# A decoder block on one core: the modulation loads of the projection stage move from SyncE's queue to GpSimd's, and a memset moves from GpSimd to VectorE

## The chip, the cores and the metric

The kernel runs on one core of one Trainium2 chip. The core has five engines with an instruction queue each: TensorE (PE in the profile; its weight loads are PEld), VectorE (DVE), ScalarE (ACT), GpSimd (POOL) and SyncE (SP). A DMA is asked for by one of the engines and carried out by 16 DMA engines. The metric is the device time in microseconds of one execution; for the kernel before it is the median of three runs.

## The reference

One layer of a hybrid decoder, 512 tokens of width 2048, all in fp32:

```python
mod = silu(c) @ w_ada + b_ada                  # six rows of 2048: shift1, scale1, gate1, shift2, scale2, gate2
h = rms_norm(x, norm1_w) * (1 + scale1) + shift1
aq, ak, av, gq, gf, gi, gg = split(h @ w_in)   # seven groups of 1024 columns
attn = rms_norm(dilated_attention(rope(norm(aq)), rope(norm(ak)), av), attn_out_norm_w)
hg = rms_norm(hgrn2(gq, gf, gi, lb), hg_norm_w) * silu(gg)
x = x + gate1 * (concat(attn, hg) @ w_out)
h2 = rms_norm(x, norm2_w) * (1 + scale2) + shift2
x = x + gate2 * (square(relu(h2 @ w_ff1)) @ w_ff2)
```

`hgrn2` is a gated linear recurrence over the tokens with 8 heads of 128 channels: its forget factors f multiply up along the tokens. The modulation `mod` is a product of one vector with a matrix of 2048 by 12288, 100 MB of weights that are read once.

## The kernel before

**Stages.** The norm of x and its scale come first, beside a first group of columns of w_in. Then the shift, then the input projection, in groups of 512 columns, with attention and the recurrence fitted between its matmuls. Then the output projection, the first products of the MLP, and two long stages with a fast matrix product. Weights come as fp32 in tiles of two k rows (`wraw`, 512 KB, L189). ScalarE rounds each to a high part (`whi`, L39), VectorE takes the rest (`wlo`, L40), and TensorE multiplies three times.

**Modulation.** One block of 512 columns of a modulation row is a `gemv` (L116): 16 loads of 128 by 512 from `w_ada` (256 KB each, tile `araw`, L123), each followed by a multiply and add on VectorE into one of two sums (`acc`, L127 and L129). `to_cols` (L138) adds the two sums (L143), lets TensorE transpose them (L149), and ScalarE sums the transposed rows. In the first stage the tiles come from pools of that stage (`early`). Later `araw` has four buffers of its own and `acc` two. `shift_through` (L744) is a gemv of `w_in` with the shift, which adds the shift's part to columns that were projected without it.

**What sets the order.** The gemvs are Python generators in a list `bgw`. `project` (L368) calls `bg_step` 1.85 times for each k of a projection, and each call writes the next load with its sum into the program. The list holds, after L836: `shift_through` of the forget gate's second half, then gate1 (`mod_rows(2)`, four gemvs), then scale and shift of the second norm (`mod_cols(4)` and `mod_cols(3)`, four each), 13 gemvs with 208 loads. gate2 (`mod_rows(5)`, L896) comes in the output projection. The order of TensorE's instructions from L831 on is that of the program. On all other engines a planner orders the instructions by simulated times, the program's order being their priority; an instruction may be put far ahead of its place in the program if its buffer is free. On the chip each engine takes its instructions in the order so fixed, so that one that waits holds up those behind it. A load waits until VectorE has read the last tile that stood in its buffer.

**The recurrence.** `hgrn_head` (L577) works through levels L = 1, 2, 4 to 256. A level multiplies z, S and f on VectorE (L597 to L608), and TensorE multiplies the z of a level (L574, L648 and others). `Sx` is S, with 512 columns, taken as pairs of halves of L columns. For L = 1 GpSimd sets all of `Sx` to 1 (L604), and VectorE copies f's odd columns over the even ones (L605). The odd columns keep the 1. There are eight heads.

**GpSimd's other work in this stage.** The rotations of q and k (L422 to L424, in `qk_norm`) and the powers for the norms (L212). In the first stage it asks for small constants, and its power for the norm of x (`rx`) is one step to the first matmuls. From the output projection on it asks for DMAs of x1 (L931) and of the MLP's operands (L1027, L1066, L1122).

Of the kernel before, what the change touches and what calls it, by code (L numbers as in the profile page):

```python
# [44 lines left out]
def hybrid_block(ctx, tc, x, c, positions, norm1_w, w_ada, b_ada, w_in, q_norm_w, k_norm_w,  # L45
                 attn_out_norm_w, hg_lb_logits, hg_norm_w, w_out, norm2_w, w_ff1, w_ff2,
                 lnc, hgmask, inv_freq, out):
    nc = tc.nc
    pe, dve, act, pool = nc.tensor, nc.vector, nc.scalar, nc.gpsimd
# [66 lines left out]
    def gemv(view, vec, col0, n=512, early=False):  # L116

        accs = [(work("acc") if early else gv.tile([P, 512], F32, name="acc"))[:, 0:n] for _ in range(2)]
        nk = 512 // n
        for k0 in range(0, NK, nk):  # L120
            raw = spare.pop(0) if early and spare else slot("araw") if early else gv.tile([P, 512], F32, name="araw", bufs=4)
            raw = raw.rearrange("p (k n) -> p k n", n=n)
            nc.sync.dma_start(raw, view[:, k0:k0 + nk, col0:col0 + n])  # L123
            for k in range(k0, k0 + nk):
                acc = accs[k % 2]
                if k < 2:
                    dve.tensor_scalar(acc, raw[:, k - k0], vec[:, k:k + 1], None, op0=ALU.mult)  # L127
                else:
                    dve.scalar_tensor_tensor(acc, raw[:, k - k0], vec[:, k:k + 1], acc, op0=ALU.mult, op1=ALU.add)  # L129
            yield  # L130
        gemv.acc = accs

    def run_all(g):
        for _ in g:
            pass
        return gemv.acc
# [23 lines left out]
    def mod_cols(kind, b, dst, nw, n=512, early=False):  # L160

        for _ in gemv(ada_v, sc, kind * D + b * n, n, early):
            yield
        nb = n // P
        d = dst[:, b * nb:(b + 1) * nb]
        yield from to_cols(gemv.acc, d)
        dve.tensor_tensor(d, d, bcol[:, kind * NK + b * nb:kind * NK + (b + 1) * nb], op=ALU.add)
        if nw is not None:
            mod_cols.last = dve.scalar_tensor_tensor(d, d, 1.0, nw[:, b * nb:(b + 1) * nb], op0=ALU.add, op1=ALU.mult)
        yield  # L170
# [39 lines left out]
    def rstd_of(dst, ss, n, inv_n):  # L210
        dve.tensor_scalar(dst, ss, inv_n, EPS, op0=ALU.mult, op1=ALU.add)
        pool.tensor_tensor(dst, dst, mhalf[:, 0:n], op=ALU.pow)  # L212
# [15 lines left out]
    def slot(name, dt=F32):  # L228
        return io.tile([P, 512], dt, name=name, tag="io")

    def work(name, dt=F32):
        return wk.tile([P, 512], dt, name=name, tag="wk")
# [113 lines left out]
    def bg_step():  # L346

        while bgw:
            try:
                return next(bgw[0])  # L350
            except StopIteration:
                bgw.pop(0)
# [85 lines left out]
    def qk(c0, name, i):  # L438
        ts = evac(project(c0, tok_mm), name)
        rs = sm.tile([P, NT, 4], F32, name=f"rs{i}", bufs=2)  # L440
        bgw.insert(0, qk_norm(ts, i, rs))
        return ts if i else (ts, rs)
# [134 lines left out]
    def hgrn_head(h, f, q, vs, ss):  # L577
# [7 lines left out]
        Sx = work("Sx")  # L585
        near = sm.tile([P, 4, 32], F32, name="near", bufs=2)

        def level(L):

            with tc.high_priority(offset=400):  # L590
                return level_ops(L)

        def level_ops(L):
            n = S // (2 * L)
            z = work("z")
            zv, kv, qv, pv, sv = (t.rearrange("p (n u l) -> p n u l", u=2, l=L) for t in (z, kk, q, f, Sx))
            if L == 1:  # L597
                dve.tensor_copy(zv[:, :, 0], kv[:, :, 0])
            else:
                dve.tensor_tensor(zv[:, :, 0], kv[:, :, 0], sv[:, :, 0], op=ALU.mult)  # L600
            dve.tensor_tensor(zv[:, :, 1], qv[:, :, 1], pv[:, :, 1], op=ALU.mult)
            if L < 256:
                if L == 1:
                    pool.memset(Sx, 1.0)  # L604
                    dve.tensor_copy(sv[:, :, 0], pv[:, :, 1])  # L605
                else:
                    dve.tensor_tensor(sv[:, :, 0], sv[:, :, 0], pv[:, :, 1, L - 1:L].broadcast_to([P, n, L]), op=ALU.mult)
                dve.tensor_tensor(pv[:, :, 1], pv[:, :, 1], pv[:, :, 0, L - 1:L].broadcast_to([P, n, L]), op=ALU.mult)  # L608
            return z
# [79 lines left out]
    def hgrn(fs, qs, vs, rs):  # L689
        ss = sm.tile([P, 4, NT], F32, name="hss", bufs=2)  # L690
        for h in range(4):
            yield from hgrn_head(h, fs[h], qs[h], vs, ss)
        rstd_of(rs.rearrange("p t h -> p (t h)"), ss.rearrange("p t h -> p (t h)"), 16, 1.0 / DH)
# [50 lines left out]
    def shift_through(col0):  # L744

        yield from gemv(win_v, s1c, col0, early=col0 < 4096 + 512)
        col = sm.tile([P, 8], F32, name="scol", bufs=2)
        yield from to_cols(gemv.acc, col[:, 0:4])
        for h in range(4):
            if col0 == 3072:  # L750
                dve.tensor_scalar(col[:, 4 + h:5 + h], col[:, h:h + 1], QS, None, op0=ALU.mult)
                sg = wk.tile([P, 512], F32, name="sg", tag="ev", bufs=2)
                act.activation(sg, hq0[h], AF.Sigmoid, scale=1.0 / QS, bias=col[:, h:h + 1])
                dve.scalar_tensor_tensor(hq0[h], hq0[h], col[:, 4 + h:5 + h], sg, op0=ALU.add, op1=ALU.mult)
            else:
                f, hd = ((f0, h), (f1, 4 + h))[(col0 - 4096) // 512]
                forget(hd, f[h], f[h], col[:, h:h + 1])
        yield
# [75 lines left out]
    while bgw:  # L834
        bg_step()
    bgw[:] = later  # L836
    tasks.append(hgrn(f0, hq0, hv0, hrs[0]))
    q0 = qk(0, "aq", 0)
    k0_ = qk(1024, "ak", 1)
# [13 lines left out]
    tasks.append(hg_out(1, gs, f1, hrs[1]))  # L853
    while bgw:
        bg_step()


    def project_out(q, rate, after):
# [542 lines left out]
def _program(arrays):  # L1401
    import concourse.bacc as bacc
    nc = bacc.Bacc("TRN2", target_bir_lowering=False, num_devices=1)
    args = [nc.dram_tensor(n, a.shape, mybir.dt.from_np(a.dtype), kind="ExternalInput").ap()
            for n, a in arrays.items()]
    args.append(nc.dram_tensor("out_0_dram", _OUTS[0][0], F32, kind="ExternalOutput").ap())
    with tile.TileContext(nc, schedule_with_timeline_sim=True) as tc:
        hybrid_block(tc, *args)
    return nc
# [10 lines left out]
```

## Time and profile before

| what | value |
|---|---|
| median of 3 runs | 2297.67 us (2294.38 to 2297.95) |
| the profiled execution | 2297.95 us, of which the trace's span is 2296.2 us |
| granted TensorE clock, mean of the span | 0.996 of full speed |
| the changed line's loads from w_ada, all stages | 384 of 256 KB, median 4.3 us from issue to landing |
| memsets of L604 | 8, from 194.2 to 636.6 us |
| TensorE busy, 500 to 600 us | 99.77 of 100 us |
| TensorE busy, 600 to 700 us | 96.78 of 100 us |

The profile is of one execution. A row of a group gives the line, the engine, the operation, the tile written and the tiles read, shapes and count, then busy time in us and mean duration in ns, then the idle time of the engine just ahead of these instructions with what ended it. A row of waits gives who waited for whom, the sum in us, how often, and the longest. A row of a timeline gives the start, the length, the engine and the instruction, with the idle time before it in brackets. SPq is SyncE's queue: its rows are instructions that ask for DMAs. In the chain of waits, which is followed back from the last instruction, a DMA's row has its issue and its time to landing.

### The profile page before, as it was taken

Reading aid. Unit: us, or ns where it says so; the run is one execution under the profiler, and the core shown is the slowest. Engines: PE = TensorE matmul, PEld = TensorE weight load, DVE = VectorE, ACT = ScalarE, POOL = GpSimd, SP = SyncE. Lnnn points to the kernel's source line nnn. Section 1 sums busy time; section 2 is a strip of 40 time slices with the busy share of each in tenths; the row PEclk is TensorE's granted clock in tenths of the full one; section 3 lists DMA queues with packets and bytes.
Section 4 is the critical chain, followed back from the end, with each engine's and each line's share of the span. In section 5 each row is a group of like instructions: output and inputs, shape, how many; then the busy total and the mean of one; then the engine's idle time right before and its main releaser. Section 6 shows DMA issues by size and latency. Waiting matters only on the chain.

```text
span 2296.2 us, 33105 instructions
## 1 busy us (share of the span) xinstructions
PE 2224.9 (97%) x11769; PEld 1824.4 (79%) x11769; DVE 1809.9 (79%) x2765; ACT 1098.2 (48%) x1950; POOL 447.3 (19%) x664
## 2 busy tenths in 40 slices
PE   4899999999999999999999999999999999999999
PEld 3787877888778888778887888888888888888887
DVE  6999777677876565668648988988897679967878
ACT  5555434433344454447544556555564333343332
POOL 1000022000230000002232323323332222222221
PEclk9999999999999999999999999999999999999999
DMA  9798455556545256746969799889889987998784
GB/s 327 254 335 315 124 177 156 177 160 207 187 151 184 68 173 225 247 152 217 367 231 383 251 344 347 298 306 386 298 328 390 339 293 260 385 344 291 278 301 164
DMA packets 262582, 598.31 MB, mean 261 GB/s; under 512 B 23220, under 2 KB 43968, under 8 KB 262416
## 3 DMA queue, kind: packets, MB, share of 16 engines
q1 hardware_dynamic: 186800, 332.54, 43.1%
q0 software_dynamic: 70720, 254.21, 30.0%
q10 hardware_dynamic: 4896, 9.44, 1.2%
q8 instruction: 93, 1.52, 0.3%
q14 instruction: 73, 0.60, 0.1%
HBM read 518.49 MB, written 77.61 MB: 260 GB/s over the span
## 4 chain that ended last, share of the span: by engine, by line
PE 60%; DVE 17%; DMA 14%; issue 6%; ACT 2%; POOL 1%; SPq 0%; DVEq 0%; ACTq 0%; POOLq 0%
PE f L1177 9%; PE f L1178 9%; PE f L1176 9%; DMA araw<-in_w_ada_dram 6%; PE prj L198 5%; PE prj L199 5%; PE prj L200 5%; DVE vlo L1161 3%; DVE acc L129 3%; DVE raw L1144 2%; PE f L208 2%; PE f L206 2%; PE f L207 2%; DMA Fl<-f_lod 2%; DVE wlo L40 2%
## 5 line engine op out<-in xcount | busy, mean ns | idle before, releaser
L1160 ACT CAST vhi<-raw 128x1024 fp32r<-128x1024 f32 x392 | 413.4, 1055 | 534.5 <-PE f L1178 416.3
L1161 DVE TENSOR_TENSOR vlo<-raw,vhi 128x1024 fp32r<-128x1024 f32 x392 | 475.5, 1219 | 153.5 <-ACT vhi L1160 152.7
L1177 PE MATMUL f<-vlo,Fh 128*128 128x512 f32 x1376 | 537.1, 390 | 3.9 <-DVE vlo L1161 3.8
L1178 PE MATMUL f<-vhi,Fl 128*128 128x512 f32 x1376 | 535.8, 389 | 0.8 <-DMA Fl<-f_lod 0.8
L1176 PE MATMUL f<-vhi,Fh 128*128 128x512 f32 x1376 | 536.1, 390 | 0.0
L39 ACT CAST whi<-wraw 128x512 fp32r<-128x512 f32 (+1 forms) x368 | 219.8, 601 | 453.2 <-PE prj L200 313.3
L198 PE MATMUL prj<-whi,hi 128*128 128x512 f32 x896 | 364.9, 407 | 1.3 <-ACT gg L701 1.3
L200 PE MATMUL prj<-whi,lo 128*128 128x512 f32 x896 | 351.4, 392 | 0.0
L199 PE MATMUL prj<-wlo,hi 128*128 128x512 f32 x896 | 351.0, 392 | 0.0
L40 DVE TENSOR_TENSOR wlo<-wraw,whi 128x512 fp32r<-128x512 f32 (+1 forms) x368 | 243.2, 665 | 120.9 <-ACT whi L39 118.3
L129 DVE SCALAR_TENSOR_TENSOR acc<-araw,sc,acc 128x512 f32<-128x512 f32 (+1 forms) x392 | 252.7, 672 | 100.5 <-DMA araw<-in_w_ada_dram 99.2
L1177 PEld LDWEIGHTS f<-vlo,Fh 128*128 128x128 f32 x1376 | 258.3, 188 | 63.3 <-DVE vlo L1161 10.0
L1178 PEld LDWEIGHTS f<-vhi,Fl 128*128 128x128 f32 x1376 | 258.3, 188 | 54.8 <-DMA Fl<-f_lod 1.6
L1176 PEld LDWEIGHTS f<-vhi,Fh 128*128 128x128 f32 x1376 | 258.3, 188 | 53.5
L1144 DVE TENSOR_TENSOR raw<-raw,raw 128x1024 f32<-128x1024 f32 x224 | 267.7, 1216 | 4.1 <-DMA raw<-in_w_ff_dram 3.9
L198 PEld LDWEIGHTS prj<-whi,hi 128*128 128x128 f32 x896 | 169.3, 189 | 36.5 <-ACT gg L701 1.6
L200 PEld LDWEIGHTS prj<-whi,lo 128*128 128x128 f32 x896 | 168.9, 188 | 36.7
L199 PEld LDWEIGHTS prj<-wlo,hi 128*128 128x128 f32 x896 | 169.5, 189 | 33.0 <-DVE wlo L40 1.0
L1122 POOL DMA_DIRECT2D Fh<-f_hid x112 | 79.0, 705 | 425.9 <-PE f L1178 410.8
L208 PE MATMUL f<-hi,wlo 128*128 128x512 f32 x256 | 99.8, 390 | 1.3 <-DVE wlo L40 1.3
L206 PE MATMUL f<-hi,whi 128*128 128x512 f32 x256 | 100.2, 391 | 0.0
L207 PE MATMUL f<-lo,whi 128*128 128x512 f32 x256 | 99.6, 389 | 0.0
(311 smaller groups left out, 2917.0 us busy)
## 6 DMA issues: line engine op xcount, KB each, us to landing
raw<-in_w_ff_dram SPq DMA_DIRECT2D x224, 512.0 KB, 9.7
araw<-in_w_ada_dram SPq DMA_DIRECT2D x384, 256.0 KB, 4.3
Fh<-f_hid POOLq DMA_DIRECT2D x112, 512.0 KB, 6.5
Fl<-f_lod POOLq DMA_DIRECT2D x112, 512.0 KB, 7.7
wraw<-in_w_in_dram SPq DMA_DIRECT2D x104, 512.0 KB, 4.1
Fh<-h_hid POOLq DMA_DIRECT2D x60, 512.0 KB, 6.6
Fl<-h_lod POOLq DMA_DIRECT2D x60, 512.0 KB, 7.5
f_hid<-part POOLq DMA_DIRECT2D x48, 512.0 KB, 7.9
```

Of the source, the lines that this page charges most:

```text
L39: nc.scalar.copy(hi, src)
L40: (eng or nc.vector).tensor_tensor(lo, src, hi.bitcast(F32), op=ALU.subtract)
L129: dve.scalar_tensor_tensor(acc, raw[:, k - k0], vec[:, k:k + 1], acc, op0=ALU.mult, op1=ALU.add)
L198: pe.matmul(banks[ti], lhsT=hi[:, ts], rhs=whi, start=first, stop=False)
L199: pe.matmul(banks[ti], lhsT=hi[:, ts], rhs=wlo, start=False, stop=False)
L200: pe.matmul(banks[ti], lhsT=lo[:, ts], rhs=whi, start=False, stop=last)
L1144: dve.tensor_tensor(dst, a, b, op=ALU.subtract)
L1160: act.copy(hi, src)
L1161: split_done.append(dve.tensor_tensor(lo, src, hi.bitcast(F32), op=ALU.subtract))
L1176: pe.matmul(banks[t], lhsT=fh[u][a][:, ts], rhs=whi[:, a], start=first, stop=False)
L1177: pe.matmul(banks[t], lhsT=fh[u][a][:, ts], rhs=wlo[:, a], start=False, stop=False)
L1178: pe.matmul(banks[t], lhsT=fl[u][a][:, ts], rhs=whi[:, a], start=False, stop=end)
```

## The change

The queue that asks for a gemv's loads becomes a variable. It is SyncE's at first, GpSimd's from the point where the list of gemvs is exchanged (after the projection that ends at L835), and SyncE's again after the list is empty (L855). And in the first level of a recurrence head VectorE writes the odd columns of `Sx`, 256 of 512, in place of GpSimd's memset of all 512.

```diff
@@ gemv
-            nc.sync.dma_start(raw, view[:, k0:k0 + nk, col0:col0 + n])
+            gemv.queue.dma_start(raw, view[:, k0:k0 + nk, col0:col0 + n])
...
+    gemv.queue = nc.sync
@@ level_ops
                 if L == 1:
-                    pool.memset(Sx, 1.0)
+                    dve.memset(sv[:, :, 1], 1.0)
                     dve.tensor_copy(sv[:, :, 0], pv[:, :, 1])
@@ the projections
     while bgw:
         bg_step()
     bgw[:] = later
+    gemv.queue = pool
     tasks.append(hgrn(f0, hq0, hv0, hrs[0]))
...
     while bgw:
         bg_step()
+
+    gemv.queue = nc.sync
```

The weight loads (L189) stay on SyncE, and so does the store of a modulation row (L183).

## The prediction

> **What bounds the kernel now.** I read the page first, for the shares of the whole run:
>
> ```profile
> PE 2224.9 (97%) x11769; PEld 1824.4 (79%) x11769; DVE 1809.9 (79%) x2765; ACT 1098.2 (48%) x1950; POOL 447.3 (19%) x664
> ```
>
> TensorE (PE) works 97% of the span, so this change can only be worth what TensorE waits for. Next I asked for one line's instructions, those of L123, to see when the loads of the change run, and cut the other views to that stretch, 270 to 770 us:
>
> ```profile
> L123 SPq DMA_DIRECT2D araw<-in_w_ada_dram x184: 327/328/985, 276.7 to 741.4; - x184
> DMA to landing us min/median/max: 2.5/3.4/5.6
> 270.00:770.00 500.00, 489.24 (x3758) 397.03 (x3757) 377.64 (x844) 217.47 (x655) 70.82 (x108) 1.00 0.55 170
> ```
>
> The third row is a stretch: its length, then busy time of PE, PEld, DVE, ACT and POOL, the clock, the share of the DMA engines and GB/s. TensorE is idle for 10.8 of the 500 us. The clock is full and the DMA engines are at 55%, so neither is short. GpSimd (POOL) works 71 us. The waits of the stretch, TensorE's first, then VectorE's (DVE), then SyncE's queue:
>
> ```profile
> PE pC L648 <- DVE z L601: 3.8, 3, 2.8
> PE pB L574 <- DVE z L601: 3.5, 2, 2.4
> PE ptq L454 <- ACT p_sb L492: 2.7, 2, 2.0
> PE pD L665 <- DVE z L601: 0.4, 1, 0.4
> DVE acc L129 <- DMA araw<-in_w_ada_dram: 63.3, 53, 3.1
> SPq L189 <- DVE wlo L40: 90.6, 42, 12.4
> SPq L123 <- DVE acc L129: 81.4, 125, 2.3
> ```
>
> TensorE waits 7.7 us (3.8 + 3.5 + 0.4) for z of the recurrence, which VectorE writes. VectorE itself stands 63.3 us in 53 waits for the very loads that the change moves, and the z queue behind such a wait. One case, from VectorE's timeline, SyncE's timeline and the chain of waits:
>
> ```profile
> 382.60 0.75 DVE L129 SCALAR_TENSOR_TENSOR acc<-araw,sc,acc 128x512 f32<-128x512 f32 x1 [2.30 <-DMA araw<-in_w_ada_dram]
> 377.06 1.13 SPq L189 DMA_DIRECT2D wraw<-in_w_in_dram  x1
> 378.29 4.28 DMA araw<-in_w_ada_dram
> 521.73 2.55 DMA araw<-in_w_ada_dram
> 664.81 2.66 DMA araw<-in_w_ada_dram
> ```
>
> The load of 378.29 is asked for right behind a weight load (377.06) and takes 4.28 us, and VectorE stands 2.30 us for it. Two that were asked for with no weight load ahead took 2.55 and 2.66. From these two facts I take a rate for the whole argument: 7.7 us of TensorE's time per 63.3 us of VectorE's, 0.12 us per us. It is an estimate that all z waits come from such stands.
>
> One cover is wide. The sums of a gemv must be done when TensorE, whose order is by hand, comes to their transposes. Of the 12 gemvs between 289 and 765 us this is the tightest:
>
> ```profile
> 515.69 0.68 DVE L143 TENSOR_TENSOR acc<-acc 128x512 f32<-128x512 f32 x1
> 525.07 0.60 PE L149 MATMUL pc<-ident,acc 128*128 128x128 f32 x4
> ```
>
> The sum ends at 516.37 and is used at 525.07, so a gemv may come 8.7 us later at no cost. Lateness hurts only through what queues on VectorE behind a load.
>
> **The change part by part.** By the code 208 loads move: 16 of the forget gate's shift (L828), 64 of gate1 (L726), 128 of the second norm's scale and shift (L727 to L729). The loads of gate2 (L896) and the shift loads before L834 stay on SyncE.
>
> *Issue.* SyncE sheds 208 x 0.328 = 68 us. I cost that at nothing: its queue in the wait view stands behind VectorE (81.4 us for the slot of the next load, 90.6 us for a weight slot), not behind its own issuing, and no row of TensorE names a weight load. GpSimd takes the issuing over. The nearest row is its own 256 KB DMA at L931:
>
> ```profile
> L931 POOL DMA_DIRECT2D x1d<-x x16: 539/539/651, 875.3 to 1022.6; - x16
> DMA to landing us min/median/max: 2.6/5.8/7.7
> wraw<-in_w_in_dram SPq DMA_DIRECT2D x68, 512.0 KB, 4.0
> ```
>
> That is 208 x 0.54 = 112 us more on an engine with 429 of 500 us free, and 0.54 - 0.33 = 0.2 us later for each load.
>
> *Landing.* Bounds: every load as quick as one alone and 0.2 later, 2.8 against the median of 3.4, or every one as slow as the median of L931, 5.8. Over 53 stands that is -32 to +127 us for VectorE, and by the rate -3.8 to +15 us for TensorE. I take a value near the low end, since L931 writes to memory amid other stores, and its fastest (2.6) is as quick as SyncE's fastest (2.5). A load in a queue of its own no longer stands behind a weight load: I put it at 3.8, between 4.28 and the 2.6 of one alone and nearer the weight load's own 4.0, because the weight bytes still pass beside it. If half of the loads gain 0.5 and the other half lose 0.2, the mean is -0.15 us, 53 x 0.15 = 8 us of VectorE, **-1.0 us**. The Trainium skill ("DMA: Bandwidth & Descriptors", section "Queues, rings and completion order") has each DMA engine take its queues in turn, a packet at a time; by that a 256 KB load would share with the weight load and not queue behind it, which is the gaining half of this term and no more. In this trace weights and modulation rows are all in one queue, so it cannot show that.
>
> *Waiting in GpSimd's queue.* A load that waits for its slot now holds up what stands behind it on GpSimd: the rotations of q and k, their powers and those of the norms. Their users come late (scores start after the next projection), so that is free up to the length of a projection. The other way round, a load waits for GpSimd's own work:
>
> ```profile
> L422 POOL TENSOR_TENSOR rot<-aq,rot_w 128x64 f32<-128x64 f32 x32 | 12.9, 436 | 56.2 <-ACT aq L406 55.9
> L212 POOL TENSOR_TENSOR hrs<-hrs,mhalf 128x16 f32<-128x16 f32 x2 | 5.8, 2898 | 67.4 <-DVE hrs L211 67.4
> L604 POOL MEMSET Sx<- 128x512 f32 x6 | 3.2, 526 | 224.8 <-PE pT L490 89.2 <-ACT whi L39 60.0 <-DVE AT L642 38.5
> 641.76 7.52 POOL L422 TENSOR_TENSOR rot<-ak,rot_w 128x64 f32<-128x64 f32 x8 [4.68 <-ACT ak L406]
> 658.60 3.36 POOL L212 TENSOR_TENSOR rs<-rs,mhalf 128x16 f32<-128x16 f32 x1
> ```
>
> Without the memsets GpSimd is busy 70.8 - 3.2 = 67.6 of 500 us, so 14% of the loads meet it: 7 of the 53 that VectorE stands for. If the order on GpSimd interleaves the two, such a load is late by an operation or a few, 0.4 to 3.4 us; I take 1.4, which makes 10 us of VectorE, **+1.2 us**. Bounds: 0, where the planner puts loads ahead, and the rival below.
>
> *The memset.* GpSimd loses eight of 0.53 us, and with them a stand of 224.8 us in front of them behind which loads would queue; that is what the second half of the edit takes away. VectorE gains eight writes of 256 elements. No such row exists; the nearest is the copy of the same shape, and the bounds are VectorE's quickest groups and an operation with two inputs of that shape:
>
> ```profile
> L605 DVE COPY Sx<-f 128x256 f32<-128x256 f32 x6 | 1.8, 307 | 0.0
> L127 DVE TENSOR_SCALAR acc<-araw,sc 128x512 f32<-128x512 f32 x23 | 11.2, 485 | 8.2 <-PE pc L149 7.3 <-DMA araw<-in_w_ada_dram 0.7
> ```
>
> 8 x 0.31 = 2.5 us of VectorE, beside 122 us in which it is idle: **+0.3 us**, at most 2.5 (if every z then is late by it), not below 0, as nobody waited for the memset (the instructions of L604 list no one).
>
> The Trainium skill ("SBUF — State Buffer", sections "SBUF: two separate sides" and "A bandwidth-pool intuition that's wrong") speaks against the change: while VectorE runs a one-input fp32 operation within SBUF, GpSimd cannot write descriptors, and a DMA of 620 ns came to 3,100. Here L605 and L127 are of that kind, 13 of 500 us, 2.6%, so 5.4 of the 208 loads would be 2.5 us late, an estimate from that page's figures: 13 us of VectorE, 1.6 of TensorE, and a time of 2301.2 and not 2299.6. The row of L931 (539 typical, 651 at most) shows none of it, and I leave it out of the sum.
>
> *The first four.* The slots for these loads are free from the start, and the planner uses that already: it asks for four rows of w_in at 36 us which nothing reads for 100 us.
>
> ```profile
> 36.06 2.85 SPq L123 DMA_DIRECT2D araw<-in_w_in_dram  x4
> 12.70 0.48 POOL L97 DMA_DIRECT2D rows<-in_hg_norm_w_dram  x1
> 27.48 1.21 POOL L212 TENSOR_TENSOR rx<-rx,mhalf 128x4 f32<-128x4 f32 x1 [14.29 <-DVE rx L211]
> 13.98 5.62 DMA xs<-in_x_dram
> 19.61 5.42 DMA xs<-in_x_dram
> 50.00:60.00 10.00, 8.04 (x38) 6.48 (x37) 10.00 (x27) 6.87 (x16) 0.00 (x0) 1.00 1.09 354
> ```
>
> On GpSimd the first free place is after 13 us, while it waits for rx, and there the DMA engines carry the x tiles on the chain. Four loads take 2.85 us of them, so the start can be 2.85 later. They leave SyncE at 36 us, but what follows then is paced by VectorE (10.00 of 10.00 at 50 us) as much as by DMA, so little is won back. Between no cost and all of it I take the middle: **+1.4 us**. A gain is not excluded where VectorE is not full, and -2.85 is the far end.
>
> The sum is -1.0 + 1.2 + 0.3 + 1.4 = +1.9 on the profiled execution (2297.95 us, 0.28 above the median of 2297.67). On the median that makes **2299.6 us**, no difference that this kernel's runs can show (they tell 0.2%, 4.6 us, from nothing).
>
> **The rivals.** *A, the stands go.* With a queue of its own a load is asked for ahead and lands alone, VectorE no longer stands, and TensorE's 7.7 us for z go: 2297.67 - 7.7 = 2290.0. For it: three of the four rows of waits name z. Against it: SyncE's stand of 81.4 us is for VectorE to free a slot, which another queue does not shorten.
>
> *B, GpSimd's order is the new wait.* If the planner puts a run of rotations ahead of loads that are due, the loads wait for the whole run, and first for q itself (55.9 us of waits in two runs). The run from 641.76 to 661.96 is 20.2 us; the four runs are 67.6 - 5.8 = 61.8 us. Each us is a stand of VectorE, which works in order: 61.8 x 0.12 = 7.4, with the first four 2297.67 + 7.4 + 1.4 = 2306.5. It decides where such a wait passes the 8.7 us that a gemv has in hand, for then TensorE stands for its transposes as well. Against it: the planner orders GpSimd by the same simulated time as the others, and most runs are short pieces with places between them.
>
> *C, nothing moves.* The loads are paced by VectorE's slots in both kernels and come at the same times: 2297.7. It cannot be told from my forecast by time, and its chance is in it.
>
> **How the numbers follow.** Forecast with C: 0.48. A: 0.27, with what lies between, over 0.2% faster. B: 0.25, over 0.2% slower. Besides the priced terms the new queues give the planner other times, and VectorE's order in the stretch changes with them; the 10.8 us that TensorE idles there may become a few more or less, which both rivals hold. The range is from a little beyond A to a little beyond B, 2288 to 2308; of the bounds it leaves out the far end of the landing (+15), which would need every load as slow as a store beside other stores.
>
> **What would show it.** Right: 208 DMAs of L123 on GpSimd at about 0.54 us, a landing of 3.3 to 3.7 us, VectorE's wait for them at 45 to 75 us in 270 to 770, and TensorE idle 9 to 14 us there. The first four stand before 27 us on GpSimd, and TensorE's first full stretch starts 0 to 3 us later. For A the z rows are gone. For B waits of L123 behind rotations or aq stand in the list of GpSimd's waits, and TensorE waits for acc at L149. Wrong I would be if the order of VectorE or ScalarE changed before 270 us, where TensorE has little in hand, by more than these terms.

## The result, and the profile after

The kernel after takes 2313.5 us (median of 6 runs, 2308.8 to 2314.5) against 2297.8 (6 runs beside them, 2294.4 to 2302.3). The ratio on record is 1.0059, 95% interval 1.0047 to 1.0070: slower by 13.6 us, between 10.8 and 16.1. Effects in this text are those of the ratio; the two medians by themselves differ by 15.7 us. The time is beyond the range of the prediction. The profiled execution took 2313.01 us, its span is 2311.2. Lines behind `gemv` stand two lower than before (L143 is now L145).

TensorE has the same work and a lower share; GpSimd is busy 102 us more. The columns are engine, busy time in us, its share of the span and the number of instructions:

```profile
PE 2227.8 (96%) x11769; PEld 1826.3 (79%) x11769; DVE 1819.1 (79%) x2773; ACT 1098.3 (48%) x1950; POOL 549.7 (24%) x864
```

Of the 15.0 us between the two spans, 12.1 are idle time of TensorE (span less busy time, 83.4 against 71.3), and 2.9 are busy time for the same instructions, at a granted clock of 0.994 against 0.996 in the mean. So most of the loss is waiting, and a smaller part is slower work.

The stretch of the recurrence comes some 15 us later, so its views are cut to 280 to 790 us. First the loads by their line, then the stretch as one row (columns as in the prediction):

```profile
L123 POOL DMA_DIRECT2D araw<-in_w_ada_dram x184: 538/538/766, 289.0 to 761.8; - x184
DMA to landing us min/median/max: 2.8/3.7/7.9
```

```profile
280.00:790.00 510.00, 493.75 (x3773) 400.18 (x3772) 388.05 (x858) 219.44 (x659) 160.78 (x286) 0.99 0.54 167
```

A load is issued in 0.54 us and lands 3.7 us after its issue began, 0.3 later than from SyncE; 0.2 of that is the longer issue. TensorE stands 16.3 of 510 us, where it stood 10.8 of 500. The waits of the stretch, TensorE's, VectorE's and GpSimd's:

```profile
PE pC L650 <- DVE z L603: 8.3, 4, 3.9
PE pB L576 <- DVE z L603: 3.8, 2, 2.2
PE pD L667 <- DVE z L603: 0.8, 1, 0.8
PE pC L656 <- DVE z L603: 0.2, 1, 0.2
DVE acc L129 <- DMA araw<-in_w_ada_dram: 70.7, 60, 3.8
POOL araw L123 <- DVE acc L129: 155.6, 101, 5.5
POOL araw L123 <- DVE acc L127: 123.1, 16, 47.6
```

TensorE's waits for z went from 7.7 to 13.1 us. GpSimd stands for VectorE to free a slot, as SyncE did before. So some 5 us arise in this stretch. The greater part is ahead of it. To see where, I set the k-th matmul of each kind in the one trace beside the k-th in the other; the table gives how much later it begins (median of the 25 matmuls from that time on, us) by its time in the trace of before:

| at (us) | 28 | 92 | 140 | 212 | 320 | 400 | 540 | 690 | 900 | 1400 | 2200 |
|---|---|---|---|---|---|---|---|---|---|---|---|
| after | 2.7 | 4.2 | 4.2 | 12.0 | 13.5 | 9.1 | 8.9 | 19.5 | 18.5 | 16.0 | 15.0 |

There are two steps ahead of 220 us: 4.2 us in the start and 8 us between 170 and 212. After that it goes up and down: down by 4 us to 400 us, up by 10 in the recurrence, and down by 4 to the end.

**The first step.** GpSimd's timeline in the start, and SyncE's load of the x tiles, after:

```profile
7.07 1.67 POOL L123 DMA_DIRECT2D araw<-in_w_in_dram  x3
10.09 0.54 POOL L123 DMA_DIRECT2D araw<-in_w_in_dram  x1 [1.35 <-DMA rw<-in_k_norm_w_dram]
30.16 1.21 POOL L214 TENSOR_TENSOR rx<-rx,mhalf 128x4 f32<-128x4 f32 x1 [16.33 <-DVE rx L213]
```

```profile
7.63 15.73 SPq L257 DMA_DIRECT2D xs<-in_x_dram  x16
```

The same of SyncE before:

```profile
7.52 13.09 SPq L255 DMA_DIRECT2D xs<-in_x_dram  x16
```

The four loads of w_in stand at 7 to 10 us, beside the x tiles. SyncE needs 2.64 us longer to get its 16 x tiles asked for, and the power for the norm of x comes at 30.16, 2.68 us later than before.

**The second step.** TensorE's stands at the end of the shift, before and then after:

```profile
214.17 1.11 PE L149 MATMUL pc<-ident,acc 128*128 128x128 f32 x4 [4.86 <-DVE acc L143]
```

```profile
202.89 0.50 PE L201 MATMUL prj<-wlo,hi 128*128 128x512 f32 x1 [3.64 <-DVE wlo L40]
226.17 1.11 PE L151 MATMUL pc<-ident,acc 128*128 128x128 f32 x4 [7.54 <-DVE acc L145]
```

The stands of after sum to 11.2 us, 6.3 more than that of before; the rest of the 8 us is not in stands of TensorE. It waits longer for sums of the shift, so I followed these sums on VectorE back to where they begin. TensorE's and VectorE's timelines at 105 to 145 us, before:

```profile
113.78 0.22 PE L769 MATMUL ps_v<-ident,posf 4*128 4x4 f32 x1
```

```profile
125.41 0.20 DVE L818 TENSOR_SCALAR cosT<-rp 128x64 f32<-128x64 f32 x1
128.49 0.54 DVE L127 TENSOR_SCALAR acc<-araw,sc 128x512 f32<-128x512 f32 x1
```

And after:

```profile
109.53 0.27 PE L770 MATMUL ps_v<-ident,rows 128*128 128x128 f32 x1
126.09 0.22 PE L771 MATMUL ps_v<-ident,posf 4*128 4x4 f32 x1
```

```profile
126.35 0.20 DVE L772 COPY cols<-ps_v 128x41 f32<-128x41 f32 x1 [0.84 <-PE ps_v L771]
141.04 0.20 DVE L820 TENSOR_SCALAR cosT<-rp 128x64 f32<-128x64 f32 x1
141.16 1.06 DVE L127 TENSOR_SCALAR acc<-araw,sc 128x512 f32<-128x512 f32 x2
```

`ps_v` (L770, L771) is a pair of small transposes, of the small vectors and of the positions, from which VectorE makes the table of the rotations (to `cosT`). Before, TensorE does them one behind the other at 113.6 to 114 us. After, the second stands behind more of the projection, at 126 us. The table follows 15.6 us later on VectorE, and the shift's next gemv (L127), which stands behind the table in VectorE's order, begins at 141.16 and not at 128.49. VectorE is then busy all of the time from 150 to 200 us in both kernels (25.00 of 25.00 in the windows 150:175 and 175:200), so nothing of that is made good before TensorE comes to the sums. That the late table is the cause is so far an argument from the order; e5_psv_first tries it.

### The profile page after: what moved, and what is told of

The parts are those of the page before. It is cut to its first block, busy times and chain, and to the rows that moved or that the text cites. A ratio compares the mean times of both kernels' runs of the same rounds, so it can differ in the third digit from the quotient of the medians.

```text
span 2311.2 us, 33191 instructions
## 1 busy us (share of the span) xinstructions
PE 2227.8 (96%) x11769; PEld 1826.3 (79%) x11769; DVE 1819.1 (79%) x2773; ACT 1098.3 (48%) x1950; POOL 549.7 (24%) x864
## 4 chain that ended last, share of the span: by engine, by line
PE 61%; DVE 14%; DMA 13%; issue 8%; POOL 2%; ACT 1%; SPq 0%; DVEq 0%; POOLq 0%; ACTq 0%
PE f L1182 11%; PE f L1183 11%; PE f L1181 11%; DMA araw<-in_w_ada_dram 8%; PE prj L200 4%; PE prj L202 4%; PE prj L201 4%; DVE vlo L1166 3%; DVE acc L129 2%; PE f L210 2%; PE f L208 2%; PE f L209 2%; DVE raw L1149 2%; DVE wlo L40 1%; PE prj L209 1%
## 5 line engine op out<-in xcount | busy, mean ns | idle before, releaser
L129 DVE SCALAR_TENSOR_TENSOR acc<-araw,sc,acc 128x512 f32<-128x512 f32 (+1 forms) x392 | 254.8, 676 | 108.5 <-DMA araw<-in_w_ada_dram 107.3
L123 POOL DMA_DIRECT2D araw<-in_w_ada_dram x192 | 105.0, 547 | 367.4 <-DVE acc L129 185.1
```

## The experiments

Theory T1: the loss comes from the first gemv of the list, whose loads run ahead into the start, and from the order that the planner then makes (T1a: through the late table; T1b: through the gemv's other 12 loads). Rival T2: from GpSimd's queue in the recurrence, by later landings and by standing in order. Rival T3: from VectorE, by the write that it got and by any change of its order. Times are medians of 5 to 12 runs beside 23 to 35 of before; intervals are those of the ratio. The table gives the shift of the matmuls against before, as above, of the profiled executions:

| at (us) | 28 | 92 | 140 | 212 | 320 | 400 | 540 | 690 | 900 | 1400 | 2200 | ratio (95%) |
|---|---|---|---|---|---|---|---|---|---|---|---|---|
| e1_memset | 0.4 | 0.7 | 0.7 | 0.6 | 0.7 | 1.3 | 1.4 | 4.3 | 2.9 | 3.0 | 3.9 | 1.0007 (0.9995 to 1.0019) |
| e2_queue | 2.8 | 4.2 | 4.2 | 12.8 | 14.7 | 10.7 | 9.7 | 13.8 | 12.5 | 17.1 | 17.0 | 1.0058 (1.0041 to 1.0075) |
| e3_first_sp | -0.2 | 0.1 | 0.4 | 0.4 | 0.6 | -3.4 | -4.1 | 3.6 | 2.9 | 5.3 | 8.4 | 1.0016 (1.0005 to 1.0028) |
| e4_held | -0.4 | -0.8 | -0.8 | 4.1 | 4.7 | 0.3 | 0.1 | 5.2 | 4.5 | 1.1 | 1.8 | 1.0026 (1.0014 to 1.0037) |
| e5_psv_first | 2.9 | 3.6 | 3.5 | 3.3 | 3.6 | -1.3 | -2.0 | 8.3 | 8.3 | 5.8 | 4.7 | 1.0022 (1.0006 to 1.0037) |
| e6_first4 | 2.5 | 3.5 | 3.5 | 9.1 | 9.0 | 11.0 | 13.2 | 15.9 | 14.7 | 13.6 | 13.3 | 1.0035 (1.0022 to 1.0048) |
| e7_other12 | 0.4 | -0.3 | -0.3 | -0.5 | -0.3 | 1.1 | 2.6 | 2.8 | 1.4 | 0.5 | 2.5 | 1.0005 (0.9992 to 1.0019) |
| e9_first2 | 1.9 | 1.5 | 1.5 | 10.6 | 12.1 | 11.0 | 11.2 | 10.9 | 9.8 | 9.7 | 8.6 | 1.0040 (1.0028 to 1.0052) |

One execution differs from the next by some us, which add up along the span, so the columns to 320 us are read first, and for the end the ratio.

### The memset alone (e1_memset)

The kernel before, with:

```diff
-                    pool.memset(Sx, 1.0)
+                    dve.memset(sv[:, :, 1], 1.0)
```

> The kernel before with the second half of the edit alone: VectorE writes the odd columns of Sx, all modulation loads stay on SyncE. Theory T1 (the 15 us come from the first gemv of the list, whose loads run ahead into the start and whose place changes VectorE's order between 90 and 220 us; the stage of the recurrence adds some 7 us that are given back in part): no part of that is here, 2297 to 2300 us, with TensorE's matmuls at the times of before up to 270 us. Rival T2 (GpSimd's queue in the recurrence itself: landings 0.35 us later, loads in order behind each other): the same 2297 to 2300. Rival T3 (VectorE's eight added writes delay z, since they come in the chain of the first level): 8 times up to 1 us, 2301 to 2306 us, with more waits of TensorE for z in 270 to 770.

2298.1 us against 2297.3. The start and the shift are as before. The waits for z of 270 to 770 us sum to 9.9 us, against 7.7. So the write costs little: 1.6 us, between -1.1 and 4.4. T3 in the sense of its forecast (2301 to 2306) is not borne out.

### The queue alone (e2_queue)

The kernel after, with:

```diff
-                    dve.memset(sv[:, :, 1], 1.0)
+                    pool.memset(Sx, 1.0)
```

> The kernel after, with GpSimd's memset of all of Sx put back: the loads move to GpSimd, VectorE gets no write. T1: the start and the shift stage as in the kernel after, first 16 loads on GpSimd, +12 us at 220 us; and the loads now queue behind the memsets' waits, so 2313 to 2325 us. T2: more than the kernel after as well, by the stands of the memsets (224.8 us in before) as far as VectorE waits for loads behind them. T3 (the memset on VectorE is what costs): less than the kernel after, 2305 to 2310 us.

2311.0 us, 2 us under T1's forecast: a ratio of 1.0058 where the kernel after has 1.0059. Both steps ahead of 220 us are there (4.2, then 12.8). The whole loss is the queue's, and leaving the memset on GpSimd makes it no worse. That loads would stand behind the memsets, for which the change has its second half, cost nothing that could be measured.

### All but the first gemv (e3_first_sp)

The kernel after, with:

```diff
-            gemv.queue.dma_start(raw, ...)
+            (nc.sync if view is win_v else gemv.queue).dma_start(raw, ...)
```

> The kernel after, but the first gemv of the list, the 16 loads from w_in for the shift of the forget gate's second half, is asked for by SyncE as before; the 192 loads from w_ada stay on GpSimd and the memset on VectorE. T1: start and shift stage as in before (matmuls within 1 us of before's times up to 270 us); what the recurrence adds (+7.3 us) and what comes back later (-4.5) stay, so 2298 to 2304 us. T2 (the queue in the recurrence is the cause): nothing or little comes back, 2308 to 2314 us, and TensorE's waits for z in 270 to 790 us stay at 13 us. If both hold in part: 2304 to 2308 us.

2300.9 us, +3.7 us (1.1 to 6.4). Sixteen loads of 208 make out 10 of the 13.6 us. In the trace the power for the norm of x is back at its time:

```profile
27.26 1.21 POOL L214 TENSOR_TENSOR rx<-rx,mhalf 128x4 f32<-128x4 f32 x1 [14.34 <-DVE rx L213]
```

The matmuls are within 0.6 us of before up to 320 us. T1 holds. T2 can have 3.7 us (6.4 by the interval), and not the 13.6.

### All loads on GpSimd, but none in the start (e4_held)

The kernel after, with:

```diff
-                pool.tensor_tensor(rot_w[:, i, j], tab, w, op=ALU.mult)
+                gemv.behind = pool.tensor_tensor(rot_w[:, i, j], tab, w, op=ALU.mult)
...
-            gemv.queue.dma_start(raw, ...)
+            with tc.issue_after(gemv.behind.ins) if gemv.queue is pool else ExitStack():
+                gemv.queue.dma_start(raw, ...)
```

> The kernel after, but every load on GpSimd is put behind GpSimd's last product of the rotation table (about 127 us), so that none is asked for in the start; all 208 stay on GpSimd. T1: the start comes back (the +4.2 us before 100 us go) and rx is ready at 27.5 us again; the shift stage keeps its loss if that is of the loads of 145 to 200 us, or loses it if it followed from the four early ones: 2301 to 2310 us. T2: the start is worth nothing at the end, 2311 to 2315 us.

2302.6 us, +6.0 us (3.2 to 8.5). With the four loads out of the start, the start comes back (-0.8 at 92 and 140 us), and with it the early table (the second transpose of `ps_v` at 113.0 us). A step of 5 us stays between 172 and 212: here all 16 loads come at 126 us and later. The two sums of this gemv, which is needed last, are added up at 202.96 us on VectorE (210.36 before), and those for which TensorE stands at 217.52 (213.43 before). So the later gemv has passed the earlier one, as T1b says. That its own queue did it, and only because all of its loads start there, fits with the order but was not tried by itself.

### The table first (e5_psv_first)

The kernel after, with:

```diff
-        pe.transpose(ps_v[:, 0:P], rows, ident)
-        pe.transpose(ps_v[:, P:P + NT], posf, ident[0:NT, 0:NT])
+        with tc.high_priority():
+            pe.transpose(ps_v[:, 0:P], rows, ident)
+            pe.transpose(ps_v[:, P:P + NT], posf, ident[0:NT, 0:NT])
```

> The kernel after, with one thing added: TensorE's two transposes of the small vectors (ps_v, L770 and L771), from which the rotation table and then the place of the shift's sums on VectorE follow, get the higher priority. Theory T1a (the start is 4 us late, the planner therefore puts the second of these transposes behind more of the projection, at 126 us and not 114, VectorE does the rotation table at 126 to 141 us, in the place of the shift's first gemv, and TensorE stands for the shift 8 us longer at 200 to 220 us): the table is ready at 125 to 130 us, the first gemv of the shift is summed from 128 to 133 us on, and 4 to 8 of the 15 us are gone: 2304 to 2309 us. Rival T1b (the 12 loads of this gemv that run on GpSimd at 145 to 200 us take the DMA's and VectorE's time from the shift, whatever the table does): 2311 to 2315 us, the loss between 130 and 220 us stays at 8 us.

2302.4 us, +5.1 us (1.4 to 8.5), a little below what T1a expected. The start is late by 3.5 us as before, and nothing is added at 212 us (3.3). TensorE's timeline and VectorE's show why:

```profile
115.04 0.22 PE L772 MATMUL ps_v<-ident,posf 4*128 4x4 f32 x1
217.95 1.12 PE L151 MATMUL pc<-ident,acc 128*128 128x128 f32 x4 [4.91 <-DVE acc L145]
```

```profile
127.07 0.21 DVE L821 TENSOR_SCALAR cosT<-rp 128x64 f32<-128x64 f32 x1
131.63 0.48 DVE L127 TENSOR_SCALAR acc<-araw,sc 128x512 f32<-128x512 f32 x1
```

The transpose is at 115.0, the table is done 14.0 us earlier than in the kernel after, the shift's gemv begins 9.5 us earlier, and TensorE's stand for its sums is the 4.9 us of before again. One priority on two small transposes takes back 1.0059 - 1.0022 = 0.0037, 8.5 us. T1b fails for the kernel after: its 12 loads still run on GpSimd here.

### Only the first four loads (e6_first4), only the other twelve (e7_other12)

The kernel before, with (in e7_other12 the condition is k0 >= 4):

```diff
-            nc.sync.dma_start(raw, ...)
+            (pool if view is win_v and col0 == 4608 and k0 < 4 else nc.sync).dma_start(raw, ...)
```

> The kernel before, with only four loads changed: the first four of the shift gemv of the forget gate's second half are asked for by GpSimd; all other loads and the memset as in before. T1a: the start is 4 us late as in the kernel after (rx's power at 30.2 us and not 27.5), the table comes late too, and the loss at 220 us is 8 to 13 us: 2305 to 2311 us. T1b: only the start, +4 us: 2300 to 2302 us.

> The kernel before, with the other 12 loads of that gemv asked for by GpSimd, the first four on SyncE. T1a: the start and the table are as before, 2296 to 2300 us. T1b (a queue of its own lets them pass the loads of the shift that is needed first): TensorE waits 4 to 6 us longer at 180 to 220 us, 2301 to 2304 us.

The four loads alone: 2308.7 us against 2299.0, by the ratio +8.0 us (5.1 to 11.0). GpSimd's and TensorE's timelines give the two steps again:

```profile
30.02 1.21 POOL L212 TENSOR_TENSOR rx<-rx,mhalf 128x4 f32<-128x4 f32 x1 [16.19 <-DVE rx L211]
```

```profile
125.40 0.22 PE L769 MATMUL ps_v<-ident,posf 4*128 4x4 f32 x1
223.31 1.12 PE L149 MATMUL pc<-ident,acc 128*128 128x128 f32 x4 [7.62 <-DVE acc L143]
```

The twelve alone: 2299.5, +1.1 us (-1.8 to 4.4), with nothing ahead of 320 us. T1a is right in both, T1b in neither.

### Two loads (e9_first2), and a control (e10_psv_before)

The kernel before, with (e9_first2; e10_psv_before is the kernel before with the priority of e5_psv_first and nothing else):

```diff
-            nc.sync.dma_start(raw, ...)
+            (pool if view is win_v and col0 == 4608 and k0 < 2 else nc.sync).dma_start(raw, ...)
```

> The kernel before with only the first two of those four loads on GpSimd, the other 14 on SyncE. Theory T1a: two loads take half of what four take from the x tiles, so the start is 1.5 to 2.5 us late (matmuls at 92 to 140 us); in the planner's order for TensorE both transposes of ps_v stand later than in before (251st and 252nd place, not 217th and 218th), so the table is late too, 2 to 8 us more at 220 us: 2300 to 2308 us. If the start is not a matter of the loads' bytes but of something else in GpSimd's list: 0 or the full 4 us at 92 us.

> The kernel before, with the higher priority for the two transposes of ps_v and nothing else; a control. T1a: the table is in time in before already (transposes at 113.8 us), so the priority brings nothing, within 2 us of before at 220 us and at the end. If the priority helps by itself, by 3 us or more, then the gain that it made in the kernel after does not show that the late table was the cause.

Two loads make the start 1.5 us late at 92 to 140 us, where four make 3.5: it grows with the number of loads. But the end is no better than with four: 2306.7 us, +9.2 (6.4 to 11.9), with 9 us added at 212 where 2 to 8 were expected, and the planner has put both transposes late, the first at 123.2 us:

```profile
123.43 0.22 PE L769 MATMUL ps_v<-ident,posf 4*128 4x4 f32 x1
224.73 1.11 PE L149 MATMUL pc<-ident,acc 128*128 128x128 f32 x4 [12.74 <-DVE acc L143]
```

TensorE stands 12.7 us for the sums. So the larger step doesn't go with the size of the delay that sets it off: it is a step of the order. The control: 2296.7 against 2296.1, ratio 1.0004 (0.9994 to 1.0014), -0.1 us at 212 us. The priority does nothing where the table was in time.

### Gate1's loads alone (e8_gate1, e11_gate1_set, e12_gate1_act)

The kernel before, with (in e12_gate1_act the queue is act; e8_gate1 and e12_gate1_act have the memset on VectorE, e11_gate1_set has it on GpSimd):

```diff
-            nc.sync.dma_start(raw, ...)
+            (pool if view is ada_v and 2 * D <= col0 < 3 * D else nc.sync).dma_start(raw, ...)
```

> The kernel before with the 64 loads of gate1 alone on GpSimd and the memset on VectorE; the 16 from w_in and the 128 of the second norm's scale and shift on SyncE. The kernels with the loads on GpSimd had won 3 to 4.5 us between 360 and 400 us, where gate1's loads run, and lost 6 between 540 and 700. If the win belongs to gate1's loads in a queue of their own: the matmuls at 400 us are 3 us earlier than in before, and 2294 to 2297 us. If both were only other places of VectorE's order (T3): anything from 2296 to 2303 us, and the waits for z in 270 to 790 us at 8 to 10 us, in other places.

> The kernel before with the 64 loads of gate1 alone on GpSimd, the memset left on GpSimd. If the loads stand behind the memsets' waits as the code says (224.8 us of stands in front of six memsets in before), gate1's loads come late and VectorE's wait for them grows: the win of 3 us at 400 us is gone, 2298 to 2304 us. If the planner puts the loads ahead of the memsets, as the kernel after with the memset put back suggests (2311.0 against 2313.5): the same as with the memset on VectorE, 2294 to 2298 us.

> The kernel before with the 64 loads of gate1 alone on ScalarE's queue and the memset on VectorE. If the win at 380 to 400 us is that of a queue apart from the weight loads, it comes with this queue as well: matmuls 3 us earlier at 400 us, 2293 to 2298 us, unless ScalarE's own work (48% busy) holds loads up. If it is only VectorE's other order: no win at 400 us, 2297 to 2303 us.

e8_gate1: 2297.1 us against 2299.0, ratio 0.9987 (0.9976 to 0.9998). e11_gate1_set: 2294.6 against 2296.1, 0.9987 (0.9978 to 0.9996). Both have the matmuls 3.4 to 3.9 us earlier at 400 us. The waits of TensorE for z in e11_gate1_set, 270 to 770 us:

```profile
PE pB L574 <- DVE z L601: 2.6, 3, 1.6
PE pC L648 <- DVE z L601: 1.9, 3, 1.2
PE pD L665 <- DVE z L601: 0.5, 1, 0.5
```

They sum to 5.0 us, not 7.7. Where the memset stands makes no difference. On ScalarE's queue there is no win: 2298.6, 1.0010 (0.9998 to 1.0022), 1.2 us late at 400 us, and TensorE waits 2.2 us for ScalarE's `aq`, a row that before lacks. So the win isn't that of any queue apart from the weights; whether it is GpSimd's queue or the order that VectorE then gets stays open. A part of it is the clock: from 380 to 400 us the granted clock is 0.91 in the trace of before and 1.00 in those of e8_gate1 and e11_gate1_set, which is 1.8 us at most. It is 1.00 in e12_gate1_act too, which is late all the same. With 3 us, under what one pair of runs shows, e11_gate1_set has the lowest median of the study, and its interval lies below 1.

### The other 128, and all 192 (e13_norm2, e14_all_ada)

The kernel before, with (in e14_all_ada the condition is 2 * D <= col0 < 5 * D):

```diff
-            nc.sync.dma_start(raw, ...)
+            (pool if view is ada_v and 3 * D <= col0 < 5 * D else nc.sync).dma_start(raw, ...)
```

> The kernel before with the 128 loads of the second norm's scale and shift alone on GpSimd; gate1's 64, the 16 from w_in and the memset as in before. With gate1's loads alone there the time fell by 0.13% (3 us); with all 192 and the memset on VectorE it rose by 0.16% (3.7 us). If the parts add up, these 128 cost 5 to 7 us: 2302 to 2304 us, with TensorE's waits for z 4 us longer between 540 and 700 us (theory T2, GpSimd's queue costs where the loads are many, by landings 0.35 us later and by standing in order). If the rise was only VectorE's order, another order in each kernel (T3): between 2296 and 2301 us, no sum of parts.

> The kernel before with all 192 loads from w_ada of the stretch on GpSimd, the 16 from w_in on SyncE and the memset left on GpSimd: the change without its first gemv and without the memset. T2: as with the memset on VectorE, 2299 to 2303 us (+0.16%), or more, since loads queue behind memsets. T3 (VectorE's order, and the eight writes on VectorE add a little): 2295 to 2299 us.

e13_norm2: 2300.5 against 2297.6, 1.0010 (1.0000 to 1.0020), +2.3 us, less than the 5 to 7 that a sum of parts from e3_first_sp asked for. e14_all_ada: 2298.0, 1.0003 (0.9992 to 1.0013). Both lie where T3 put them and below T2's forecast. All 192 loads on GpSimd cost nothing that can be seen (0.7 us, -1.8 to 3.0), with their landing at a median of 3.7 us and z waits of 7.8 us. T2 falls. What stays of the 3.7 us is small; that it goes with VectorE's order is not shown. The 3.0 us between e14_all_ada and e3_first_sp are the memset's, in intervals that overlap; e2_queue beside the kernel after gives 0.2 for the same edit. I put the memset at 0 to 3 us.

## Why the prediction was wrong

The result, +13.6, is made of the late table (8.5, by e5_psv_first) and of the 5.1 that are left there: 3.5 of them are the late start, and 1 to 2 us hold the recurrence and the memset. The intervals of these parts are some us wide, and the parts don't add up exactly: the four loads alone cost 8.0, and everything but the first gemv 3.7.

*The first four* is the step that failed. Its price was +1.4 us, at most 2.85, and it cost 8.0 (5.1 to 11.0) by itself. The loads stand at 7 us, earlier than was thought (13). The delay at its place was right (2.68 us for the norm of x), nothing was won back, and 4.2 were late at 92 us. What the term left out is larger: it took the rest of the stretch to 270 us as a fixed sequence that is shifted. It is planned anew. A delay of 1.5 to 4 us there put small transposes behind a row of matmuls and cost 6 to 9 us more at 212 us, through VectorE, which has no slack from 150 to 200 us. The prediction's last sentence names this ("if the order of VectorE or ScalarE changed before 270 us") without a price. It quotes VectorE as full from 50 to 60 us and says nothing of 150 to 200, where it is as full, and where work that is moved ahead of the shift's sums is paid for by them.

Of the signs named for being right, the issue, the landing (3.7, at the edge) and VectorE's wait (70.7) came. TensorE's idle time in the stretch (16.3, not 9 to 14) and the late start (4.2, not 0 to 3) did not.

*Issue* was right: 538 ns by the row, on an engine with room, and no TensorE row in the recurrence for the weights. No run shows that SyncE's relief was worth anything.

*Landing* had the wrong sign: 3.7 and not 3.3. Of the 184 loads before, 94 had one weight load in flight when their issue ended and took 4.04 us on average, 3.71 from the end of their issue; after, 107 had one and took 4.32, 3.78 from the end. So a queue apart did not let a load pass a weight load. The Trainium skill ("DMA: Bandwidth & Descriptors", section "Queues, rings and completion order") has the DMA engines take their queues in turn by the packet; these averages show no gain of it for a 256 KB load beside a 512 KB one. The price for the end was small all the same: the z waits are 8.9 us in e2_queue and e3_first_sp and 7.8 in e14_all_ada, against 7.7, so 0 to 1.2 us for 0.3 us a load. (From the moment at which VectorE frees a slot to the landing of the next load in it, a load is even 0.8 us later: a median of 4.2 us in the kernel after and 4.3 in e14_all_ada, against 3.4.)

*The descriptors*, which I left out of the sum: the 184 issues took 538, 538 and 766 ns (least, median, most). No issue of the length that the Trainium skill ("SBUF — State Buffer", section "A bandwidth-pool intuition that's wrong") gives for a blocked GpSimd is among them, in a stretch where VectorE does the copies and first products of that kind. It is not a hard trial: 15 of the issues overlap a copy, a memset or a product with a scalar on VectorE, and these took 538 to 766 ns. Here it was right to leave the term out.

*Waiting in GpSimd's queue* was +1.2. The wait is there, about as often as was put, but no cost can be seen. I set the end of each product on VectorE beside the start of the load that takes its slot. SyncE began to ask 0.03 us after the slot was free. GpSimd takes 0.30 us, and 25 of 180 loads (14%) start 0.6 to 5.4 us after it, behind rotations and powers, as here:

```profile
372.81 0.81 DVE L129 SCALAR_TENSOR_TENSOR acc<-araw,sc,acc 128x512 f32<-128x512 f32 x1
374.33 2.33 POOL L424 TENSOR_TENSOR rot<-ak,rot_w 128x64 f32<-128x64 f32 x4
377.80 1.11 POOL L123 DMA_DIRECT2D araw<-in_w_ada_dram  x2
380.83 0.75 DVE L129 SCALAR_TENSOR_TENSOR acc<-araw,sc,acc 128x512 f32<-128x512 f32 x1 [1.79 <-DMA araw<-in_w_ada_dram]
```

The slot is free at 373.62, the load starts at 377.80, and VectorE stands 1.79 us for it. Over the 25, VectorE stands 13 times, 16 us at most by this wait, where 10 were put. The list of waits doesn't show it, since GpSimd is at work meanwhile. e14_all_ada has 24 such loads and costs 0.7 us (-1.8 to 3.0), so the price is lost in the noise. *Rival B* has the wait right and the size wrong: no load was held for more than 5.4 us, under the 8.7 that a gemv has in hand, and the side came out for another reason, ahead of 270 us. The rotations' 55.9 us of waits for `aq` are gone, which fits with loads that stand ahead of them and hold the queue until `aq` is there; that was not tried by itself.

*The memset*, +0.3 and at most 2.5: eight writes of 272 ns, and 0 to 3 us by the pairs above. The size can't be told better than that.

*The rate* of 0.12 us of TensorE's time for one of VectorE's stands was a mean, and I used it for a change. Over the 16 kernels VectorE's stands for these loads (L127 and L129) go from 60.9 to 70.7 us and the z waits from 5.0 to 13.1; a line through them has a slope of 0.56 (correlation 0.78). By that line, an estimate, the kernel after's 6.7 us more of stands go with 4 of its 5.4 us more of z waits.

*Rival A* may have a core that is right: with gate1's loads alone on GpSimd the waits for z fall to 5.0 and the time by 3 us, though why stays open. It didn't decide here, since the other parts took more.

## What to carry to other kernels

When a DMA moves to an engine that is idle early, ask first how far ahead its buffers let it be issued, and hold it behind an instruction of the time at which it is wanted: four loads of 256 KB in a start in which the DMA engines are busy for 98% of the first 50 us, wanted more than 100 us later, cost more here than 192 loads in their right place (8.0 against 0.7 us). Where a planner orders the engines, a moved operation changes the order of everything after it; price not only the operation but the few small instructions on which a full engine's order hangs, and give those a priority. Cost a change at the margin (what the next microsecond of waiting does), not by the mean of waits over a stretch.

## What else the runs showed

Executions of the same kernel differ with the granted TensorE clock. Of the 116 runs of the kernel before that stand beside the experiments, those with a mean granted clock of 0.993 have a median of 2303.8 us (6 runs), 0.994 has 2299.8 (14), 0.995 has 2298.5 (44), 0.996 has 2295.6 (40) and 0.997 has 2294.7 (10): some 2.3 us for each 0.001. It is as much as most of the effects above, so that a single execution can't tell them, and the ratios of many can.

The clock has a share in the effects themselves. The mean over the runs is 0.9937 for the kernel after and 0.9942 to 0.9944 for the three others with the late table (e2_queue, e6_first4, e9_first2), against 0.9951 to 0.9957 for the kernel before. At 2.3 us for each 0.001 that makes 2 to 4 us of their losses, an estimate; whether the lower clock follows from the longer stands is not shown. TensorE's idle time counts no slow matmul, and it shows the same split: 83.4 us in the kernel after, 79.8 to 81.7 in those three, 76.1 in e5_psv_first, and 66.3 to 72.4 in the kernel before and all others.

The two queues differ little for such loads: 2.66 us from the end of the issue to the landing on SyncE's when no weight load was in flight (90 loads), 2.79 on GpSimd's (73 loads). A load takes 0.2 us longer to ask for on GpSimd, which is the larger part of the difference from the start of the issue (3.00 against 3.34 us).
